# Block sums of weights on GpSimd, operand loads on its queue, and a final norm in columns, in a one-core decoder layer

## The chip, the cores and the metric

The kernel runs on one core of a Trainium2 chip. The metric is device time in microseconds (us) of one execution. All matrix work is single precision, emulated: each operand is split into a high and a low part, and TensorE does three products (high·high, high·low, low·high) for one.

## The reference, cut to what matters

One inference step of one layer on 520 tokens (512 of a prompt and 8 decode tokens), model width 2048, MLP width 8192:

```python
def block(x, ...):
    y, new = mixer(rmsnorm(x, w['g_mix']), ...)          # RG-LRU beside mLSTM; y = [...] @ w_out
    x = x + y
    x = x + cross_attn(rmsnorm(x, w['g_xattn']), mk, mv, w)   # w_cq, softmax over 256 memory tokens, w_co
    hf = rmsnorm(x, w['g_ffn'])
    x = x + jnp.square(jax.nn.relu(hf @ w['w_up'])) @ w['w_down']
    return x, new                                         # then a final rmsnorm of x
```

The 8 decode tokens have states of their own; the keys and values of the memory are results too.

## The kernel before, in words

A first part, to about 612 us, computes the input projection and the two recurrences. The rest is a row of matrix products with activations transposed (128 rows of features by 520 tokens): `out` (w_out), the memory's keys, `cq`, the memory's values, attention, `co`, `up`, and four groups of `down` (`d`).

**Strassen units.** `out`, `cq`, `co`, `up` and the `d` groups go through `strassen`, in 8, 8, 8, 32 and 4 x 8 = 88 units. A unit makes 256 output columns: its weights are four blocks A11, A21, A22, A12 of 128x1024, and it takes seven products, p0 to p6, in place of eight. The weight operand of each is a block or a sum of blocks, made by `weights(k, p)`:

- p0: A11
- p1: SS = A21 + A22, in a new tile
- p2: SS - A11 (and here also A21 becomes A11 - A21)
- p3: A12
- p4: the new A21
- p5: SS becomes A12 - SS
- p6: A22

The sums are `sub`, line 834, one VectorE instruction each. A product is 24 matmuls of 128x260 (line 955) into one of three PSUM banks, `acca`, `accb`, `accc`. The weight operand of product n + 2 (`LOOK`) is prepared while product n runs: `split_weights` makes `whi` on ScalarE (line 101) and `wlo` on VectorE (line 102). Blocks are loaded by `fetch` (line 889) on SP's queue, into a pool of seven tiles, which the sums share. A load waits until the last reader of its tile is done, and SP's queue goes in order.

**Operands.** The activation side has seven slots of two batches, each a high and a low tile. `batch_load` reads a batch from DRAM (line 858, on SP's queue as well), ScalarE casts it to the high part (line 859), and VectorE subtracts for the low part (line 854). The DRAM copies (`tdcq`, `tdup`, `tdd`) are written by `spill` (line 845) on GpSimd's queue, POOL. The last units of a stage are written straight into the operand tiles by `set_tail` (line 874).

**Results of a product.** `onto` adds a bank to an output tile (line 962, VectorE). In up, `blocks` copies it to `t` (line 973, ScalarE) or adds it (line 971, VectorE); after p6 come relu and square (lines 1355 and 1356), the operand's sums (`mixed`, line 834, on `w`), and the spill. `residual` stores the residual stream to `dx[2]` (line 995, POOL).

**scale_back.** While up runs, a side task computes two reciprocals by Ln and Exp (`negative_inverse`, lines 1318 to 1321; on ScalarE each Ln and Exp loads a table here), then takes the eight tiles of the residual stream, loads each (line 1341), multiplies it twice on VectorE (line 1345), and stores it (line 1346, POOL). It works with two tiles.

**Order.** A Tile scheduler puts the recorded instructions in order for each engine by priorities; preparation of weights, and evacuation, run ahead by 100 places. Each engine and each DMA queue then goes through its instructions in that order.

Of the kernel before, what the change touches and what calls it, by code (L numbers as in the profile page):

```python
# [9 lines left out]
F32 = mybir.dt.float32  # L10
F32R = mybir.dt.float32r
AF = mybir.ActivationFunctionType
# [33 lines left out]
def tile_trunk(ctx: ExitStack, tc: tile.TileContext, a, o):  # L46
# [71 lines left out]
    def start(gen, rate=None):  # L118

        tasks.append([gen, rate, 0.0])  # L120
# [677 lines left out]
    def rest():  # L798
# [22 lines left out]
        def tl(tag, shape, dt=F32):  # L821
            return stage[tag].tile(list(shape), dt, tag=tag, name=nm(tag))
# [10 lines left out]
        def sub(out, x, y, op=ALU.subtract):  # L833
            V.tensor_tensor(out=out, in0=x, in1=y, op=op)
# [20 lines left out]

        def batch_load(key, s, b, n=4):
            hi, lo = op_tile(), op_tile()
            load(lo[:, 0:n].bitcast(F32), td[key][b][:, s, 0:n])
            S.copy(hi[:, 0:n], lo[:, 0:n].bitcast(F32))  # L859
            lo_of(lo[:, 0:n], lo[:, 0:n].bitcast(F32), hi[:, 0:n])  # L860
            sets.setdefault((key, s), []).append((hi, lo))
# [449 lines left out]

        def up_enter():
            enter("d", x=2, r=1, t=2, w=2)()
            start(scale_back())

        def negative_inverse(y, t, v):

# [3 lines left out]
            V.scalar_tensor_tensor(out=y, in0=t, scalar=2.0, in1=y, op0=ALU.subtract, op1=ALU.mult)  # L1321

        def scale_back():
            for _ in range(16):
                yield

            va, vb = tl("x", (P, 2, T)), tl("x", (P, 2, T))
            v, y, t = va[:, 0], va[:, 1], vb[:, 0]
            mean_of(v)
            st["rphi"] = tl("r", (P, T))  # L1330
            negative_inverse(y, t, scl)
            V.scalar_tensor_tensor(out=st["rphi"], in0=y, scalar=-1.0, in1=v, op0=ALU.mult, op1=ALU.mult)
            yield
            negative_inverse(y, t, v)
            V.scalar_tensor_tensor(out=scl, in0=y, scalar=-1.0, in1=scl, op0=ALU.mult, op1=ALU.mult)
            yield
            for u in range(KB // 2):
                for _ in range(6):
                    yield
                x = tl("x", (P, 2, T))  # L1340
                load(x, dx[2][u])
                for _ in range(6):
                    yield
                for i in range(2):
                    V.tensor_tensor(out=x[:, i], in0=x[:, i], in1=st["rphi"], op=ALU.mult)
                store(dx[3][u], x)
# [12 lines left out]

        X = []  # L1360

        def down_load(u):
            x = tl("x", (P, 2 * T))
# [6 lines left out]
        def down_evac(u, p, box, last):  # L1370
            onto([st["X", u][:, 0], st["X", u][:, 1]], p, box["out"])
            if p == 6 and not last:
                store(dx[3][u], st["X", u])
            if last and p == 6:
                for n in (2 * u, 2 * u + 1):
                    if n == 0:
                        st["sc2"] = op_tile((P, T), F32)
                        V.scalar_tensor_tensor(out=st["sc2"], in0=scl, scalar=1.0 / D, in1=scl,
                                               op0=ALU.mult, op1=ALU.mult)
                        st["ss"] = tl("ss", (P, T))  # L1380
                        S.activation(st["ss"], X[n], AF.Square)
                    else:
                        for c in HALF:
                            sq = ax()[:, 0:HT]
                            S.activation(sq, X[n][:, c], AF.Square)
                            V.tensor_tensor(out=st["ss"][:, c], in0=sq, in1=st["ss"][:, c], op=ALU.add)

        def final():

            r, v, s_, q_ = (op_tile((P, T), F32) for _ in range(4))  # L1390
            for n in range(2, KB, 3):
                S.activation(X[n], X[n], AF.Copy, scale=pc(C_FIN, n))
            for c in HALF:
                ps = ax()
                PE.matmul(ps[:, 0:HT], ones, st["ss"][:, c], start=True, stop=True)
# [3 lines left out]
            S.activation(s_, s_, AF.Exp, scale=-0.5)  # L1399
# [3 lines left out]
            V.scalar_tensor_tensor(out=r, in0=q_, scalar=1.5, in1=s_, op0=ALU.add, op1=ALU.mult)  # L1403
            axs.close()
            with tc.tile_pool(name="pfin", bufs=1, space=PSUM, reuse_waits="tile") as pf:
                rp = pf.tile([P, 2, 512], F32, tag="rp", name="rp")[:, :, 0:HT]
                S.copy(rp, halves(r))
                for n in range(KB):
                    x = X[n]
                    if n % 3 == 2:  # L1410
                        G.tensor_tensor(out=x, in0=x, in1=r, op=ALU.mult)
                    else:
                        V.scalar_tensor_tensor(out=halves(x), in0=halves(x), scalar=pc(C_FIN, n), in1=rp,
                                               op0=ALU.mult, op1=ALU.mult)
                    (S.dma_start if n % 2 else load)(o["y"][n], x)
# [241 lines left out]
```

## Time and profile before

| | |
|---|---|
| median of three runs | 2793.49 us (2789.72 to 2793.79) |
| profiled execution | 2796.05 us, of which the span is 2794.2 |
| TensorE busy | 2665.4 us, 95% of the span |
| VectorE busy | 2245.1 us, 80% |
| ScalarE busy | 1437.9 us, 51% |
| GpSimd busy | 107.5 us, 4% |
| HBM read, written | 427.45 MB, 120.51 MB |

The stages by time in the trace: out from about 612 us, the memory's keys and cq from about 830, co to about 1415, up from there to about 2096, d to about 2769, then the final norm. In rows of the profile PE is TensorE, PEld its weight loads, DVE VectorE, ACT ScalarE, POOL GpSimd, SP the queue that only issues transfers. "DMA op<-tdup" is a load of an operand, "DMA raw<-in_w_up" a fetch of a weight block, "SPq L889" the time of SP's queue at that line. A clock of 1.00 is TensorE's full speed.

### The profile page before, as it was taken

The page shows a single profiled execution, that of the slowest core. Times are in us where ns is not written, and L with a number is a line of the kernel's source. Part 1 is how long each engine was busy: PE and PEld are TensorE (multiplying, and loading weights), DVE is VectorE, ACT ScalarE, POOL GpSimd, SP SyncE. Part 2 cuts the span into 40 slices and gives each one's busy share as a digit, 9 for nine tenths or more (in the row PEclk, how much of TensorE's full clock was granted, in tenths as well). Part 3 has the DMA queues.
Part 4 walks back from the last instruction along what each step waited for, and adds up shares of the span by engine and source line. Part 5 has one row for each costly group of instructions (what it writes and reads, how often), then busy time and mean ns, then how long its engine had stood idle before and what let it go on. Part 6 is the DMA issues. An engine that isn't in the chain of part 4 may idle for free.

```text
span 2794.2 us, 52079 instructions
## 1 busy us (share of the span) xinstructions
PE 2665.4 (95%) x21146; PEld 2613.6 (94%) x21146; DVE 2245.1 (80%) x3203; ACT 1437.9 (51%) x2114; POOL 107.5 (4%) x164
## 2 busy tenths in 40 slices
PE   8999999999999999889969999999999999999996
PEld 8999999999999998669969999999998999999996
DVE  7777788658887898789878777777878887978886
ACT  6445556525455467675455455545554353434543
POOL 0000000030000000000000000000000000000000
PEclk9999999999999999999989999999999999999998
DMA  4666643377676579976666545454457465654632
GB/s 169 196 211 213 196 148 94 99 272 275 220 247 227 202 229 324 335 256 210 198 216 228 174 145 168 151 162 157 159 198 258 164 238 168 222 186 161 223 109 81
DMA packets 178857, 551.24 MB, mean 197 GB/s; under 512 B 23725, under 2 KB 33645, under 8 KB 178617
## 3 DMA queue, kind: packets, MB, share of 16 engines
q1 hardware_dynamic: 152808, 453.61, 48.9%
q0 software_dynamic: 24080, 90.50, 9.0%
q8 instruction: 166, 2.72, 0.4%
q10 hardware_dynamic: 1728, 3.80, 0.4%
q14 instruction: 75, 0.61, 0.1%
HBM read 427.45 MB, written 120.51 MB: 196 GB/s over the span
## 4 chain that ended last, share of the span: by engine, by line
PE 36%; issue 16%; DMA 4%; DVE 2%; ACT 2%; POOL 1%; SPq 0%; POOLq 0%; DVEq 0%; ACTq 0%
PE acca L955 19%; PE accc L955 9%; PE accb L955 5%; PE mv L1202 2%; PE ax L185 1%; DMA op<-dq 1%; DMA x<-dx 1%; DMA dx<-x 1%; DVE wlo L102 1%; DVE op L854 0%; DMA kv<-in_V 0%; ACT kv L1159 0%; PE row L1129 0%; DMA tdup<-w 0%; DMA op<-tdup 0%
## 5 line engine op out<-in xcount | busy, mean ns | idle before, releaser
L955 PE MATMUL acca<-op,whi 128*128 128x260 f32 x5632 | 1037.3, 285 | 33.2 <-ACT t L973 10.3
L955 PEld LDWEIGHTS acca<-op,whi 128*128 128x128 f32 x5632 | 877.7, 190 | 38.1 <-ACT whi L101 11.9
L955 PE MATMUL acca<-op,wlo 128*128 128x260 f32 x2816 | 801.9, 285 | 4.5 <-DVE wlo L102 4.4
L101 ACT CAST whi<-raw 128x1024 fp32r<-128x1024 f32 x388 | 406.8, 1050 | 426.7 <-PE acca L955 148.8
L955 PEld LDWEIGHTS acca<-op,wlo 128*128 128x128 f32 x2816 | 535.4, 190 | 6.1 <-DVE wlo L102 6.1
L102 DVE TENSOR_TENSOR wlo<-raw,whi 128x1024 fp32r<-128x1024 f32 x388 | 473.5, 1222 | 77.4 <-ACT whi L101 73.7
L955 PE MATMUL accc<-op,whi 128*128 128x260 f32 x2816 | 518.5, 284 | 1.4 <-ACT whi L101 1.3
L101 ACT CAST whi<-raws 128x1024 fp32r<-128x1024 f32 x264 | 276.9, 1049 | 369.2 <-PE accc L955 110.0
L166 PE MATMUL mm<-xa,whi 128*128 128x260 f32 x2624 | 432.9, 286 | 11.1 <-ACT whi L101 8.3
L955 PEld LDWEIGHTS accc<-op,whi 128*128 128x128 f32 x2816 | 438.1, 189 | 2.7 <-ACT whi L101 1.8
L102 DVE TENSOR_TENSOR wlo<-raws,whi 128x1024 fp32r<-128x1024 f32 x264 | 322.9, 1223 | 121.5 <-ACT whi L101 120.8
L955 PE MATMUL accc<-op,wlo 128*128 128x260 f32 x1408 | 400.2, 284 | 0.9 <-DVE wlo L102 0.9
L166 PEld LDWEIGHTS mm<-xa,whi 128*128 128x128 f32 x2624 | 365.0, 190 | 13.7 <-ACT whi L101 8.3
L955 PE MATMUL accb<-op,whi 128*128 128x260 f32 x1408 | 262.1, 286 | 8.4 <-ACT op L859 4.6
L955 PEld LDWEIGHTS accc<-op,wlo 128*128 128x128 f32 x1408 | 266.5, 189 | 1.3 <-DVE wlo L102 1.2
L166 PE MATMUL mm<-xa,wlo 128*128 128x260 f32 x1312 | 266.2, 284 | 0.0
L955 PEld LDWEIGHTS accb<-op,whi 128*128 128x128 f32 x1408 | 219.6, 190 | 9.8 <-ACT op L859 4.8
L166 PEld LDWEIGHTS mm<-xa,wlo 128*128 128x128 f32 x1312 | 203.9, 190 | 0.7 <-DVE wlo L102 0.5
L955 PE MATMUL accb<-op,wlo 128*128 128x260 f32 x704 | 200.8, 285 | 0.4 <-DVE wlo L102 0.3
L854 DVE TENSOR_TENSOR op<-op,op 128x1040 fp32r<-128x1040 f32 (+3 forms) x136 | 159.9, 1180 | 36.5 <-ACT op L859 22.0
L859 ACT CAST op<-op 128x1040 fp32r<-128x1040 f32 (+1 forms) x112 | 111.9, 1007 | 90.1 <-DMA op<-tdd 55.0
L101 ACT CAST whi<-wraw 128x1024 fp32r<-128x1024 f32 x82 | 85.5, 1043 | 122.8 <-PE mm L166 99.9
(386 smaller groups left out, 3355.0 us busy)
## 6 DMA issues: line engine op xcount, KB each, us to landing
raw<-in_w_up SPq DMA_DIRECT2D x128, 512.0 KB, 3.4
raw<-in_w_down SPq DMA_DIRECT2D x100, 512.0 KB, 4.1
wraw<-in_w_in SPq DMA_DIRECT2D x79, 512.0 KB, 4.0
tdd<-w POOLq DMA_DIRECT2D x32, 1040.0 KB, 6.3
x<-dx SPq DMA_DIRECT2D x56, 520.0 KB, 5.5
op<-tdd SPq DMA_DIRECT2D x56, 520.0 KB, 5.2
dx<-x POOLq DMA_DIRECT2D x48, 520.0 KB, 4.9
raw<-in_w_mk SPq DMA_DIRECT2D x32, 512.0 KB, 5.3
```

The costliest lines, as they stand in the source:

```text
L101: S.copy(hi, raw)
L102: V.tensor_tensor(out=lo, in0=raw, in1=hi.bitcast(F32), op=ALU.subtract)
L166: PE.matmul(ps[:, hf, 0:HT], w[:, j, :], x[:, HALF[hf]], start=(k == 0 and wi == 0), stop=(k == n - 1 and wi == 2))
L185: PE.matmul(out, u, v, start=first and i == 0, stop=last and i == 2)
L854: V.tensor_tensor(out=lo, in0=src, in1=hi.bitcast(F32), op=ALU.subtract)
L859: S.copy(hi[:, 0:n], lo[:, 0:n].bitcast(F32))
L955: PE.matmul(out, u[:, k], x[:, j], start=(new and k == 0 and i == 0), stop=(k == 7 and i == 2), skip_group_check=not new)
L1202: PE.matmul(st["mv"][i], x[:, ms], u[:, j], start=(k == 0 and wi == 0), stop=(k == KB - 1 and wi == 2))
```

## The change

1. `batch_load` for cq and up issues on POOL's queue in place of SP's (14 loads each).
2. In `weights`, the sum A11 - A21 moves from p2 on VectorE to p3 on GpSimd, and A12 - SS from p5 on VectorE to p3 on GpSimd, two products sooner. Both are still 128x1024 with two SBUF inputs. VectorE has 3003 rows after, 3175 before; POOL 373 and 169.
3. `scale_back` starts at p6 of unit 2 of up, its first ScalarE instructions behind that unit's square, in place of the entry of up and 16 steps. One reciprocal comes ahead of the mean.
4. The final norm's factor is computed on [128, 5] columns (one number a token): one-column matmuls against `ones`, five small VectorE operations, Sqrt in place of Ln and Exp with its table loaded early by a dummy, and six matmuls that spread the columns over 128x520 in PSUM (`rp`). VectorE's eleven multiplications read `rp`; GpSimd's five read a copy. The columns `scol`, `sc2`, `esc` are made in the last group of d.

```diff
-            load(lo[:, 0:n].bitcast(F32), td[key][b][:, s, 0:n])
+            (store if key in ("cq", "up") else load)(lo[:, 0:n].bitcast(F32), td[key][b][:, s, 0:n])
...
             elif p == 2:
-                sub(R(A21), R(A11), R(A21))
                 sub(R(SS), R(SS), R(A11))
-            elif p == 5:
-                sub(R(SS), R(A12), R(SS))
+            elif p == 3:
+                G.tensor_tensor(out=R(A21), in0=R(A11), in1=R(A21), op=ALU.subtract)
+                G.tensor_tensor(out=R(SS), in0=R(A12), in1=R(SS), op=ALU.subtract)
...
         def up_enter():
             enter("d", x=2, r=1, t=2, w=2)()
-            start(scale_back())
...
         def scale_back():
-            for _ in range(16):
-                yield
...
+            with tc.issue_after(st["mark"].ins):
+                negative_inverse(y, t, scl)
             mean_of(v)
-            st["rphi"] = tl("r", (P, T))
-            negative_inverse(y, t, scl)
...
-                S.activation(w[:, 0:4], t, AF.Square)
+                ins = S.activation(w[:, 0:4], t, AF.Square)
+                if u == 2:
+                    st["mark"] = ins
+                    start(scale_back())
...
-                        st["sc2"] = op_tile((P, T), F32)
...
+                        columns(ps, [scl], ident)
...
+                        with tc.issue_after(ins.ins):
+                            S.activation(cols[:, 3], ones[:, 0:NCH + 1], AF.Sqrt)
...
-            for c in HALF:
-                ps = ax()
-                PE.matmul(ps[:, 0:HT], ones, st["ss"][:, c], start=True, stop=True)
-                V.tensor_tensor(out=v[:, c], in0=ps[:, 0:HT], in1=st["sc2"][:, c], op=ALU.mult)
-            V.tensor_tensor(out=v, in0=v, in1=esc, op=ALU.add)
-            S.activation(s_, v, AF.Ln)
-            S.activation(s_, s_, AF.Exp, scale=-0.5)
-            S.activation(q_, s_, AF.Square)
-            V.tensor_tensor(out=s_, in0=s_, in1=scl, op=ALU.mult)
+            columns(ps, [st["ss"]], ones)
+            V.tensor_tensor(out=v, in0=ps[:, 0:NCH + 1], in1=st["sc2"], op=ALU.mult)
+            V.tensor_tensor(out=v, in0=v, in1=st["esc"], op=ALU.add)
+            S.activation(s_, v, AF.Sqrt)
+            V.reciprocal(s_, s_)
+            V.tensor_tensor(out=q_, in0=s_, in1=s_, op=ALU.mult)
...
-                S.copy(rp, halves(r))
+                            PE.matmul(rp[:, h, o_:o_ + b_ - a_], rc[:, c:c + 1].to_broadcast([P, P]),
+                                      ident[:, a_ - c * CH:b_ - c * CH], start=True, stop=True)
...
+                S.copy(halves(r), rp)
```

Where it moves instructions, by the order on each engine. First the entry of up: SP's queue before, from the last fetches of co. The names are tiles with their numbers; `tdup_120` and `tdup_121` are the two batches of up's operands in DRAM, `raw` the weight blocks.

```order
L889 DMA raw_16217<-in_w_up 128x1024
L889 DMA raw_16219<-in_w_up 128x1024
L858 DMA op_16208<-tdup_120 128x1040
L889 DMA raw_16300<-in_w_up 128x1024
L858 DMA op_16213<-tdup_121 128x780
L889 DMA raw_16509<-in_w_up 128x1024
L858 DMA op_16252<-tdup_120 128x1040
L889 DMA raw_16544<-in_w_up 128x1024
L858 DMA op_16257<-tdup_121 128x780
L858 DMA op_16291<-tdup_120 128x1040
L858 DMA op_16296<-tdup_121 128x780
L889 DMA raw_16546<-in_w_up 128x1024
```

The same place on POOL's queue after; `dx` rows are stores of the residual stream, line 845 is the spill of co's unit 6, L911 and L912 are the two sums, of co's unit 7 (`raws_16128`) and of up's units 0 and 1.

```order
L858 DMA op_16207<-tdup_120 128x1040
L996 DMA dx_6_152<-x_15970 128x1040
L845 DMA tdup_121<-w_16159 1024x1x260
L912 TENSOR_TENSOR raws_16128<-raw_16038,raws_16128 128x1024
L858 DMA op_16212<-tdup_121 128x780
L911 TENSOR_TENSOR raw_16216<-raw_16171,raw_16216 128x1024
L858 DMA op_16253<-tdup_120 128x1040
L858 DMA op_16258<-tdup_121 128x780
L858 DMA op_16292<-tdup_120 128x1040
L996 DMA dx_7_153<-x_16203 128x1040
L858 DMA op_16297<-tdup_121 128x780
L858 DMA op_16334<-tdup_120 128x1040
```

The loads stood between fetches of weight blocks; now they stand between stores and sums, and SP's queue has the fetches alone. Further on, an SS sum stands ahead of slot 3's second batch, and an A21 sum ahead of slot 4's.

Second, POOL while scale_back runs, before (units 0 to 4 of up; the `dx` rows are scale_back's stores):

```order
L1346 DMA dx_1_155<-x_17707 128x1040
L845 DMA tdd_0_122<-w_16729 1024x1x260
L1346 DMA dx_2_156<-x_18091 128x1040
L1346 DMA dx_3_157<-x_18490 128x1040
L1346 DMA dx_4_158<-x_18887 128x1040
L1346 DMA dx_5_159<-x_19281 128x1040
L845 DMA tdd_0_122<-w_16956 1024x1x260
L1346 DMA dx_6_160<-x_19669 128x1040
L1346 DMA dx_7_161<-x_20069 128x1040
L845 DMA tdd_0_122<-w_17198 1024x1x260
```

and after (from the sum for unit 4):

```order
L911 TENSOR_TENSOR raw_17234<-raw_17190,raw_17234 128x1024
L1345 DMA dx_0_154<-x_17476 128x1040
L1345 DMA dx_1_155<-x_17859 128x1040
L912 TENSOR_TENSOR raws_17394<-raw_17304,raws_17394 128x1024
L845 DMA tdd_0_122<-w_17425 1024x1x260
L911 TENSOR_TENSOR raw_17466<-raw_17432,raw_17466 128x1024
L1345 DMA dx_2_156<-x_18258 128x1040
L1345 DMA dx_3_157<-x_18656 128x1040
L1345 DMA dx_4_158<-x_19048 128x1040
L1345 DMA dx_5_159<-x_19437 128x1040
L912 TENSOR_TENSOR raws_17623<-raw_17533,raws_17623 128x1024
L845 DMA tdd_1_123<-w_17654 1024x1x260
```

The stores come some four units later, and the sum for p5 of unit 5 stands behind four of them.

Third, VectorE in a steady unit before (unit 3 of up into unit 4; `w` rows are the sums of the operand that is spilled):

```order
L102 TENSOR_TENSOR wlo_17399<-raws_17396,whi_17398 128x1024
L834 TENSOR_TENSOR raws_17396<-raws_17396,raw_17205 128x1024
L102 TENSOR_TENSOR wlo_17439<-raws_17396,whi_17438 128x1024
L834 TENSOR_TENSOR w_17427<-w_17427 128x520
L834 TENSOR_TENSOR raws_17396<-raw_17303,raws_17396 128x1024
L834 TENSOR_TENSOR w_17427<-w_17427 128x260
L102 TENSOR_TENSOR wlo_17474<-raw_17303,whi_17473 128x1024
L834 TENSOR_TENSOR w_17427<-w_17427 128x260
L102 TENSOR_TENSOR wlo_17504<-raw_17240,whi_17503 128x1024
L834 TENSOR_TENSOR raws_17626<-raw_17469,raw_17471 128x1024
L834 TENSOR_TENSOR raw_17469<-raw_17434,raw_17469 128x1024
L102 TENSOR_TENSOR wlo_17539<-raws_17396,whi_17538 128x1024
```

and after, some units on:

```order
L102 TENSOR_TENSOR wlo_17856<-raws_17853,whi_17855 128x1024
L834 TENSOR_TENSOR raws_17853<-raws_17853,raw_17661 128x1024
L102 TENSOR_TENSOR wlo_17897<-raws_17853,whi_17896 128x1024
L834 TENSOR_TENSOR w_17886<-w_17886 128x520
L834 TENSOR_TENSOR w_17886<-w_17886 128x260
L102 TENSOR_TENSOR wlo_17934<-raw_17763,whi_17933 128x1024
L834 TENSOR_TENSOR w_17886<-w_17886 128x260
L102 TENSOR_TENSOR wlo_17964<-raw_17698,whi_17963 128x1024
L834 TENSOR_TENSOR raws_18085<-raw_17927,raw_17929 128x1024
L102 TENSOR_TENSOR wlo_17995<-raws_17853,whi_17994 128x1024
```

The SS sum behind the split of p2 and the A21 sum behind the next unit's p1 sum are gone from VectorE; what is left stands in the same order.

More of the change, by code (lines that the diff above doesn't have):

```diff
@@ L1398, in final @@
-            S.activation(s_, v, AF.Ln)
-            S.activation(s_, s_, AF.Exp, scale=-0.5)
-            S.activation(q_, s_, AF.Square)
-            V.tensor_tensor(out=s_, in0=s_, in1=scl, op=ALU.mult)
+            v, s_, q_, rc = (cols[:, 3 + i] for i in range(4))
+            ps = ax()
+            columns(ps, [st["ss"]], ones)
+            V.tensor_tensor(out=v, in0=ps[:, 0:NCH + 1], in1=st["sc2"], op=ALU.mult)
+            V.tensor_tensor(out=v, in0=v, in1=st["esc"], op=ALU.add)
+            S.activation(s_, v, AF.Sqrt)
@@ L1402, in final @@
+            V.reciprocal(s_, s_)
+            V.tensor_tensor(out=q_, in0=s_, in1=s_, op=ALU.mult)
             V.scalar_tensor_tensor(out=q_, in0=q_, scalar=-0.5, in1=v, op0=ALU.mult, op1=ALU.mult)
-            V.scalar_tensor_tensor(out=r, in0=q_, scalar=1.5, in1=s_, op0=ALU.add, op1=ALU.mult)
+            V.scalar_tensor_tensor(out=rc, in0=q_, scalar=1.5, in1=s_, op0=ALU.add, op1=ALU.mult)
+            V.tensor_tensor(out=rc, in0=rc, in1=st["scol"], op=ALU.mult)
             axs.close()
             with tc.tile_pool(name="pfin", bufs=1, space=PSUM, reuse_waits="tile") as pf:
-                rp = pf.tile([P, 2, 512], F32, tag="rp", name="rp")[:, :, 0:HT]
-                S.copy(rp, halves(r))
+                rp = pf.tile([P, 2, 512], F32, tag="rp", name="rp")
+                for c in range(NCH):
+                    for a_, b_ in ((c * CH, min((c + 1) * CH, HT)), (max(c * CH, HT), (c + 1) * CH)):
+                        if a_ < b_:
+                            h, o_ = a_ // HT, a_ - a_ // HT * HT
+                            PE.matmul(rp[:, h, o_:o_ + b_ - a_], rc[:, c:c + 1].to_broadcast([P, P]),
+                                      ident[:, a_ - c * CH:b_ - c * CH], start=True, stop=True)
+                PE.matmul(rp[:, 1, TP - HT:T - HT], rc[0:NB, NCH:NCH + 1].to_broadcast([NB, P]),
+                          ident[0:NB, 0:NB], start=True, stop=True)
+                rp = rp[:, :, 0:HT]
+                S.copy(halves(r), rp)
```

14 lines of the change are left out of this document (11 added, 3 removed).

## The prediction

> **What bounds the kernel.** I read the page first, then what TensorE waits for, then busy time by stretch, and last the chain and the queues at the entry of the up-projection, where the waits led. From the page:
>
> ```profile
> span 2794.2 us, 52079 instructions
> PE 2665.4 (95%) x21146; PEld 2613.6 (94%) x21146; DVE 2245.1 (80%) x3203; ACT 1437.9 (51%) x2114; POOL 107.5 (4%) x164
> ```
>
> TensorE works for 95% of the span, and the diff takes no matmul off it but in the tail. All that can be won is the 129 us in which it stands still. TensorE's waits (total, times, longest, in us), the three that matter here:
>
> ```profile
> PE acca L955 <- ACT t L973: 10.3, 2, 10.1
> PE accb L955 <- ACT op L859: 4.6, 1, 4.6
> PE ax L257 <- DVE ss L1002: 2.1, 1, 2.1
> ```
>
> The first two are single waits of 10.1 and 4.6, so they belong to one place and not to each unit. By stretch (length, then busy time of PE, PEld, DVE, ACT, POOL):
>
> ```profile
> 1748.00:1950.00 202.00, 202.00 (x1684) 202.00 (x1684) 156.33 (x171) 103.94 (x131) 8.46 (x10) 1.00 0.49 158
> 1405.00:1470.00 65.00, 41.69 (x279) 39.83 (x278) 49.31 (x64) 38.01 (x51) 1.62 (x3) 0.82 0.57 208
> 1260.00:1380.00 120.00, 120.00 (x1000) 119.91 (x999) 107.96 (x141) 60.98 (x74) 8.45 (x12) 1.00 0.63 206
> ```
>
> In the steady up stage (first row) TensorE has no gap, and VectorE is free for 46 of 202 us: work taken from it there is worth nothing. The same holds in the out-projection of cross-attention (third row), where VectorE is 90% busy. The entry of up (second row) loses 23 us of TensorE, and its granted clock, 0.82 there against 1.00, stretches what is left. Starts of the last product of a unit, from the timeline (first row, last unit of co) and the chain (up units 0, 2, 4, 5):
>
> ```profile
> 1411.65 0.48 PE L955 MATMUL acca<-op,whi 128*128 128x260 f32 x2 [1.77 <-DVE x L962]
> ```
>
> ```profile
> 1460.98 4.68 PE acca L955 x24
> ...
> 1505.54 6.01 PE acca L955 x48
> ...
> 1546.13 5.77 PE acca L955 x48
> ...
> 1566.31 5.77 PE acca L955 x48
> ```
>
> An undisturbed unit is 1566.31 - 1546.13 = 20.18. Unit 0 of up takes 49.33, so 29.2 are lost; units 1 and 2 take 44.56 against 40.36, so 4.2 more. Part of the 29.2 is the clock: the product at 1460.98 lasts 4.68, and an undisturbed one, half of the 5.77 of two, 2.88.
>
> **The change, part by part.** *Operand loads on POOL's queue.* The chain at that entry:
>
> ```profile
> 1396.77 9.31 DMA tdup<-w
> 1406.22 3.07 DMA op<-tdup
> ...
> 1437.90 1.24 DVE wlo L102
> 1439.15 0.33 SPq L889
> ...
> 1440.06 5.26 DMA op<-tdup
> 1445.34 1.06 ACT op L859
> ...
> 1448.02 1.28 ACT L1318
> ...
> 1453.40 5.12 DMA x<-dx
> ```
>
> The load that lands at 1445.34 had its source since 1406. It stood in SP's queue behind a weight fetch (L889), whose buffer came free when VectorE ended a `wlo` at 1439.15. That is the 10.1 wait: ScalarE does the cast at 1445.34 first, then the copy of `t` on which TensorE waits. On POOL's queue no load stands behind a fetch. It stands behind other things: the store of `dx2[7]`, which needs the last residual of co (about 1415), and GpSimd's sums, of which the order has five among the fourteen loads or just ahead. Costs from the groups of VectorE and GpSimd (count, busy us, mean ns):
>
> ```profile
> L834 DVE TENSOR_TENSOR raw<-raw,raw 128x1024 f32<-128x1024 f32 x81 | 98.9, 1222 | 1.1
> L834 DVE TENSOR_TENSOR raws<-raw,raws 128x1024 f32<-128x1024 f32 x81 | 98.9, 1221 | 0.7
> L854 DVE TENSOR_TENSOR op<-op,op 128x1040 fp32r<-128x1040 f32 x99 | 122.0, 1238 | 22.3 <-ACT op L859 17.7 <-ACT op L1226 4.6
> ```
>
> ```profile
> L1411 POOL TENSOR_TENSOR x<-x,op 128x520 f32<-128x520 f32 x5 | 6.2, 1274 | 175.3 <-DVE op L1403 175.3
> ```
>
> GpSimd's 1274 for 520 elements scale to 2.5 us for 1024. Five sums are 12.5, and fourteen issues at 0.55 (the store rows below) some 8: 20 us of POOL work, which fits a window of 35. What is late next is VectorE. It is busy 49.3 of 65 us, which makes 37.4 in the 49.33 of unit 0; five sums (6.1) and scale_back's first rows (some 3) leave it, so 28 remain, and of its present 12 us of waits for casts and landings (49.33 - 37.4) I let it keep 8 to 10, since the casts of 14 loads and the co tail stay. So unit 0 would take 36 to 38 from 1411.65, and its last product would start at 1448 to 1450, against 1460.98. I take **-12**; ends: -6 (the loads gain only the 5.26 landing and a cast, since POOL releases them late too) and -18 (half of VectorE's remaining waits go as well; at -29 nothing would be lost, which the casts and subtractions of 14 loads exclude). The loads of cq's operands have the same form; from the waits above the ax row's 2.1 is before the loads and stays. **-1.5**, ends -4 and +1.
>
> *scale_back later.* It started in unit 0 of up and now starts in unit 2, after its activation. The 4.2 lost in units 1 and 2 should go, and a similar loss can come back in units 3 to 6, where GpSimd's sums stand between the stores. Chain rows before, one round of a pair of tiles, and two of the stores on POOL:
>
> ```profile
> 1479.55 1.23 DVE x L1345 x2
> ...
> 1481.07 5.96 DMA dx<-x
> 1487.10 3.45 DMA x<-dx
> ```
>
> ```profile
> 1474.97 0.55 POOL L1346 DMA_DIRECT2D dx<-x  x1 [0.62 <-DVE x L1345]
> 1490.03 0.53 POOL L1346 DMA_DIRECT2D dx<-x  x1 [8.43 <-DVE x L1345]
> ```
>
> A round is 1.2 + 0.3 + 6.0 + 3.4 and a wait for VectorE: 15 us from pair to pair. VectorE's order now puts the multiplications of the pairs half a unit apart, 10 us, between the `wlo` of the running products; each VectorE row behind a multiplication that waits for its load is late by up to 3 to 5 us. Three rounds, of which VectorE's 23% of free time absorbs part: **+4**, ends 0 and +10. With the -4.2, **0**.
>
> *The sums on GpSimd.* 88 units, two sums each (81 of each kind in the rows above, seven more of each in the units that take other buffers): 176 x 1.22 = 215 us leave VectorE, 176 x 2.5 = 440 us come to GpSimd, 5 us of a 20.18 us unit. Beside a full TensorE the first is worth nothing. Does the second come late? Rows of a steady unit, from VectorE's and TensorE's timelines:
>
> ```profile
> 1652.37 1.23 DVE L102 TENSOR_TENSOR wlo<-raws,whi 128x1024 fp32r<-128x1024 f32 x1 [1.89 <-ACT whi L101]
> ...
> 1655.60 1.22 DVE L102 TENSOR_TENSOR wlo<-raw,whi 128x1024 fp32r<-128x1024 f32 x1
> ```
>
> ```profile
> 1658.60 0.28 PE L955 MATMUL accb<-op,wlo 128*128 128x260 f32 x1
> ```
>
> SS can be overwritten once the split of product 2 has read it, 1653.6; 2.5 later is 1656.1. Its own split (product 5) begins two products on, some 2.4 us after that, so the sum is early. The A21 sum stands behind the unit's spill, almost a unit ahead of its use. The split of product 3, which ran in between at 1655.60, is needed by 1658.60. **0**, +2 for entries of stages where slack is short; ends -3 and, if VectorE and GpSimd keep each other out, +35 (rival).
>
> The Trainium skill speaks against this part: in "SBUF — State Buffer", section "Who interferes with whom", a VectorE instruction with two SBUF inputs contends with a GpSimd instruction that reads SBUF, and the second of them waits for the whole of the first. Every `wlo` and sum here is of that kind. By that rule the 5.0 us of GpSimd per unit would be taken from VectorE's 202.00 - 156.33 free us in ten units; no row of before shows the two side by side, since L1411 runs beside a multiplication with one SBUF input.
>
> *Tail.* Before, the norm goes over 128x520 tiles; now over five columns:
>
> ```profile
> 2770.12 1.15 PE L1395 MATMUL ax<-ss,ones 128*128 128x260 f32 x4 [1.41 <-DVE ss L1386]
> ...
> 2773.15 1.28 ACT L1399 ACT_TABLE_LOAD   x1
> ...
> 2778.49 7.42 DVE L1413 SCALAR_TENSOR_TENSOR x<-x,par,rp 128x520 f32<-128x520 f32 x11 [0.66 <-ACT rp L1407]
> ```
>
> The old path was 2778.49 - 2770.12 = 8.4. Rows for the new one, from the timeline at the entry of cq and from VectorE's and ScalarE's groups:
>
> ```profile
> 838.55 3.33 PE L257 MATMUL ax<-ones,ss 128*128 128x1 f32 x24 [2.06 <-DVE ss L1002]
> ```
>
> ```profile
> L1051 DVE SCALAR_TENSOR_TENSOR nv<-ax,ne 128x5 f32<-128x5 f32 x1 | 0.2, 159 | 0.0
> ```
>
> ```profile
> L206 ACT ACTIVATE nrs<-nv 128x5 f32<-128x5 f32 x1 | 0.2, 208 | 0.6 <-DVE nv L1051 0.6
> ```
>
> The new path: columns of one tile instead of two, 1.7 (half of 3.33) plus 0.3 to release VectorE; seven small VectorE operations and one of ScalarE at 0.16 to 0.21 each, 1.3, and 0.6 for two changes of engine; six broadcast matmuls some 1.2 (estimate, as the six column matmuls less their wait); release 0.3. Sum 5.4, so **-3**; ends -1.5 and -4.5. GpSimd gets its copy about as long after VectorE as before, and its 6.25 us end before VectorE's 7.42.
>
> *Others.* The d stage's loads stay on SP; fewer VectorE rows at its entries, -1, ends -2 and +2.
>
> Sum: -12 - 1.5 + 0 + 2 - 3 - 1 = -15.5. The profiled execution took 2796.05 (span 2794.2 and 1.9 around it) and lies 2.6 above the median of 2793.49; against the median 2778.
>
> **Rivals.** *The two engines keep each other out (slower).* Place: each of 88 units, around product 3. If a sum starts at 1653.6 and VectorE's next two-input rows wait until 1656.1, the `wlo` that began at 1655.60 comes behind one delayed row and ends at 1657.4 to 1659, against 1658.60: from nothing to 0.4 us per unit. From 15.5/88 = 0.18 us per unit on, the gain is gone; at 0.4, +35: 2813. In co it would be worst, since 107.96 - 6 x 2.44 + 6 x 5.0 = 123 us of 120 would be occupied. No row speaks for it, and none excludes it, since the two kinds of instruction do not meet before. Against: in up 15.6 - 2.4 + 5.0 = 18.2 of 20.18 still fit, and splits are made two products ahead. By the rule of "SBUF — State Buffer" the keeping out itself is certain, and only whether the slack holds is open.
>
> *The loads only change queues.* dx_7's store waits for the last residual of co, and a GpSimd sum for a split: loads behind them come late as they did behind fetches. Entry gain 5 instead of 12, scale_back +3: 2788, no change to be seen.
>
> *scale_back blocks.* The stores of four tiles stand ahead of SS of unit 5 on POOL; if a multiplication waits a whole round, that sum, its split and product 5 are late, 5 us twice: 2788 likewise.
>
> *The entry empties.* All of -18, tail -4.5, cq -4: 2768.
>
> **How the numbers follow.** 0.2% of 2793, 5.6 us, is about what a measurement can tell from no change. Forecast (2770 to 2787): 0.62. Loads or scale_back give half back (2785 to 2791): 0.14, half of it within 0.2%. The entry empties: 0.08. Lock or another loss in steady units: 0.16, of which 0.04 merely eats the gain (2788 to 2799) and 0.12 is slower. Faster 0.62 + 0.06 + 0.08 = 0.76; within 0.2% 0.12; slower 0.12. The range, 2767 to 2797, leaves out most of the lock rival and the last bit below.
>
> **What would show it.** Right: the 10.1 wait on `t` L973 gone; unit 0 of up 36 to 39 us long; no TensorE gap from 1748 to 1950's counterpart, GpSimd's sums 2.5 us each; VectorE's last eleven multiplications beginning about 5.5 after the last sum of squares. Wrong: `wlo` rows whose length or start shifts by GpSimd's 2.5 and a TensorE wait on `wlo` L102 that grows with the number of units; loads on POOL issued later than 1440's counterpart; waits of TensorE around units 4 and 5 of up.

## The result, and the profile after

The change made the kernel slower: 2857.75 us, median of 2851.5 to 2859.4, against 2791.6 (2781.53 to 2793.79); ratio 1.0244, interval 1.0224 to 1.0264. The profiled execution has a span of 2857.6, 63.4 more than before. The page after, the lines that answer to those of before:

```profile
span 2857.6 us, 52462 instructions
PE 2690.3 (94%) x21178; PEld 2633.3 (92%) x21178; DVE 2333.4 (82%) x3030; ACT 1436.5 (50%) x2112; POOL 596.2 (21%) x368
```

VectorE lost 176 sums of 1.22 us, 215 us of work, and its busy time grew by 88 us. TensorE computes nothing more to speak of and is busy 25 us longer. What it waits for after:

```profile
PE acca L956 <- DVE x L963: 29.5, 15, 4.5
PE acca L956 <- ACT t L974: 13.7, 3, 10.2
PE acca L956 <- DVE wlo L102: 11.8, 9, 2.8
PE accc L956 <- DVE wlo L102: 9.5, 7, 2.8
```

The wait of ten microseconds on `t` is still there. New is the first row: 15 waits of some two microseconds each for `x` L963, the addition of a product to its output tile (before, two waits, 2.2 us in all). By stretch, co's units, the entry of up, and the steady up stage:

```profile
1260.00:1456.00 196.00, 172.11 (x1331) 169.40 (x1330) 161.89 (x185) 90.25 (x120) 51.26 (x35) 0.94 0.54 185
1456.00:1510.00 54.00, 36.42 (x238) 35.07 (x239) 36.69 (x45) 28.78 (x40) 11.53 (x13) 0.78 0.42 152
1620.00:2141.00 521.00, 521.00 (x4344) 521.00 (x4342) 432.92 (x388) 272.39 (x341) 179.35 (x78) 1.00 0.50 161
```

Steady up is full as before, with 179 us of GpSimd beside it. Co was full before and isn't now. VectorE's groups say why. Before:

```profile
L102 DVE TENSOR_TENSOR wlo<-raw,whi 128x1024 fp32r<-128x1024 f32 x388 | 473.5, 1222 | 77.4 <-ACT whi L101 73.7
L962 DVE TENSOR_TENSOR x<-acca,x 128x260 f32<-128x260 f32 x192 | 81.5, 425 | 25.4 <-PE acca L955 21.5 <-DMA x<-dx 2.9
L834 DVE TENSOR_TENSOR w<-w 128x260 f32<-128x260 f32 x96 | 40.7, 424 | 0.1
L1002 DVE TENSOR_TENSOR ss<-ss,sq 128x1040 f32<-128x1040 f32 x14 | 17.3, 1236 | 0.0
```

and after (lines one higher):

```profile
L102 DVE TENSOR_TENSOR wlo<-raw,whi 128x1024 fp32r<-128x1024 f32 x388 | 576.7, 1487 | 61.1 <-ACT whi L101 59.9
L834 DVE TENSOR_TENSOR w<-w 128x260 f32<-128x260 f32 x96 | 105.1, 1095 | 1.1
L1003 DVE TENSOR_TENSOR ss<-ss,sq 128x1040 f32<-128x1040 f32 x14 | 41.4, 2959 | 0.0
L963 DVE TENSOR_TENSOR x<-acca,x 128x260 f32<-128x260 f32 x192 | 80.9, 421 | 27.1 <-PE acca L956 26.5
```

The same instructions on the same shapes take 1.2 to 2.6 times as long where both inputs lie in SBUF. The one that reads a PSUM bank (`acca`) and one SBUF tile, the last row, takes what it took.

One unit of co shows the whole mechanism. The rows are timelines: start, duration, engine, line, names, and the idle time before it. VectorE in a unit of co before:

```profile
1356.03 1.24 DVE L1002 TENSOR_TENSOR ss<-ss,sq 128x1040 f32<-128x1040 f32 x1
1357.18 0.42 DVE L962 TENSOR_TENSOR x<-acca,x 128x260 f32<-128x260 f32 x1
```

VectorE, GpSimd and TensorE after, each by itself:

```profile
1389.75 0.42 DVE L834 TENSOR_TENSOR w<-w 128x260 f32<-128x260 f32 x1
1390.09 3.43 DVE L1003 TENSOR_TENSOR ss<-ss,sq 128x1040 f32<-128x1040 f32 x1
1393.45 0.42 DVE L963 TENSOR_TENSOR x<-acca,x 128x260 f32<-128x260 f32 x1
```

```profile
1389.97 2.45 POOL L912 TENSOR_TENSOR raws<-raw,raws 128x1024 f32<-128x1024 f32 x1 [1.34 <-issue]
```

```profile
1391.74 0.28 PE L956 MATMUL accc<-op,wlo 128*128 128x260 f32 x1
1394.01 0.48 PE L956 MATMUL acca<-op,whi 128*128 128x260 f32 x2 [2.00 <-DVE x L963]
...
1395.34 0.42 PE L956 MATMUL acca<-op,wlo 128*128 128x260 f32 x1
...
1398.37 0.28 PE L956 MATMUL acca<-op,wlo 128*128 128x260 f32 x1
```

GpSimd's SS sum starts 0.12 us ahead of the addition of squares and ends at 1392.42. The addition, 1.24 us by itself, ends at 1393.52, 1.10 behind GpSimd's end: it was shut out until then. This is so throughout: of the fourteen additions of squares, the eleven that start beside a running sum take 3.42 to 3.43 us and end 1.10 behind its end, and the other three keep 1.24. Behind the addition in VectorE's queue stands `x` L963, which empties the bank that TensorE's product 2 writes next. TensorE stands for 2.00 us. Soon after it is slow: the first and last rows of the fence have matmuls of 0.28, the one at 1395.34 has 0.42, and so it goes until about 1398.1. The granted clock, the third number from the end, was 1.00 in the 3.41 us that hold the gap and 0.50 in the next 3.42:

```profile
1391.25:1394.66 3.41, 1.42 (x12) 1.24 (x11) 3.41 (x3) 1.05 (x1) 1.99 (x2) 1.00 0.45 139
1394.66:1398.08 3.42, 3.42 (x18) 3.42 (x17) 3.04 (x4) 0.00 (x0) 0.27 (x1) 0.50 0.99 382
```

That product takes 4.64 us by its first start and last end where its neighbours take 3.05. 2.0 + 1.6 is 3.6 us a unit, and most units of out and co are 23.9 us after, 20.2 to 20.3 before. Two gaps of the same length in co, 2.08 before 1292.77 and 1.99 before 1323.58, have no slow product behind them (one unit there is 22.4); the last section says what sets them apart.

Where the time went, by stage: in microseconds from the start of product 3 in one unit to that in another (d to the end of the last product), worked out from TensorE's timeline of one profiled execution each; the other kernels are the experiments below. The first part is the same program in all and varies by 7.5, which is how far single executions can be trusted. Those of the first experiment and of the tied kernel ran 4 and 9 us below their medians.

| stretch | before | after | sums on VectorE | sums only | squares through PSUM | scale_back tied |
|---|---|---|---|---|---|---|
| first part, to out | 675.3 | 671.7 | 670.2 | 670.2 | 672.9 | 667.8 |
| out | 224.5 | 244.8 | 221.9 | 249.6 | 229.2 | 221.5 |
| cq and attention | 358.5 | 363.8 | 357.8 | 366.6 | 360.3 | 357.5 |
| co, units 0 to 7 | 142.8 | 162.3 | 143.0 | 166.0 | 144.9 | 142.8 |
| co 7 to up 3 (entry) | 116.1 | 111.9 | 104.1 | 118.9 | 106.4 | 101.9 |
| up 3 to 6 | 60.5 | 73.9 | 68.6 | 60.5 | 75.1 | 61.4 |
| up 6 to 31 | 504.3 | 504.0 | 504.3 | 504.0 | 504.0 | 504.3 |
| d | 686.7 | 701.9 | 680.9 | 700.2 | 702.9 | 680.0 |
| behind the last product | 25.5 | 23.3 | 22.9 | 25.5 | 23.3 | 23.3 |

### The profile page after: what moved, and what is told of

Its sections match the earlier page's. It is cut to its first block, busy times and chain, and to the rows that moved or that the text cites. A ratio compares the mean times of both kernels' runs of the same rounds, so it can differ in the third digit from the quotient of the medians.

```text
span 2857.6 us, 52462 instructions
## 1 busy us (share of the span) xinstructions
PE 2690.3 (94%) x21178; PEld 2633.3 (92%) x21178; DVE 2333.4 (82%) x3030; ACT 1436.5 (50%) x2112; POOL 596.2 (21%) x368
## 5 line engine op out<-in xcount | busy, mean ns | idle before, releaser
L956 PE MATMUL acca<-op,whi 128*128 128x260 f32 x5632 | 1054.9, 288 | 59.4 <-DVE x L963 29.5
L956 PEld LDWEIGHTS acca<-op,whi 128*128 128x128 f32 x5632 | 892.6, 193 | 66.7 <-ACT whi L101 27.5
L956 PE MATMUL acca<-op,wlo 128*128 128x260 f32 x2816 | 810.5, 288 | 11.9 <-DVE wlo L102 11.8
L102 DVE TENSOR_TENSOR wlo<-raw,whi 128x1024 fp32r<-128x1024 f32 x388 | 576.7, 1487 | 61.1 <-ACT whi L101 59.9
L956 PEld LDWEIGHTS acca<-op,wlo 128*128 128x128 f32 x2816 | 543.4, 193 | 14.1 <-DVE wlo L102 14.0
L102 DVE TENSOR_TENSOR wlo<-raws,whi 128x1024 fp32r<-128x1024 f32 x264 | 394.3, 1494 | 127.7 <-ACT whi L101 126.9
L912 POOL TENSOR_TENSOR raws<-raw,raws 128x1024 f32<-128x1024 f32 x81 | 209.4, 2585 | 579.9 <-DVE wlo L102 442.7
L911 POOL TENSOR_TENSOR raw<-raw,raw 128x1024 f32<-128x1024 f32 x81 | 226.9, 2802 | 423.0 <-DVE raws L834 338.7
L854 DVE TENSOR_TENSOR op<-op,op 128x1040 fp32r<-128x1040 f32 (+3 forms) x136 | 183.8, 1355 | 47.6 <-ACT op L859 32.0
```

The costliest lines, as they stand in the source:

```text
L102: V.tensor_tensor(out=lo, in0=raw, in1=hi.bitcast(F32), op=ALU.subtract)
L854: V.tensor_tensor(out=lo, in0=src, in1=hi.bitcast(F32), op=ALU.subtract)
L911: G.tensor_tensor(out=R(A21), in0=R(A11), in1=R(A21), op=ALU.subtract)
L912: G.tensor_tensor(out=R(SS), in0=R(A12), in1=R(SS), op=ALU.subtract)
L956: PE.matmul(out, u[:, k], x[:, j], start=(new and k == 0 and i == 0), stop=(k == 7 and i == 2), skip_group_check=not new)
```

## The experiments

Theory A: a VectorE instruction with two SBUF inputs and a GpSimd instruction that reads SBUF keep each other out; out and co lose since the SS sum falls beside the addition of squares with a bank's evacuation behind it. Rival B: the loss comes from POOL's queue, which now carries loads, stores and sums.

**Sums back on VectorE, the rest of the change kept** (the base of most others):

```diff
             elif p == 2:
+                sub(R(A21), R(A11), R(A21))
                 sub(R(SS), R(SS), R(A11))
-            elif p == 3:
-                G.tensor_tensor(out=R(A21), in0=R(A11), in1=R(A21), op=ALU.subtract)
-                G.tensor_tensor(out=R(SS), in0=R(A12), in1=R(SS), op=ALU.subtract)
+            elif p == 5:
+                sub(R(SS), R(A12), R(SS))
```

> The changed kernel with both sums back on VectorE at their old places; loads on POOL's queue, the late scale_back and the tail in columns stay. Theory A (GpSimd's sums shut out VectorE's two-input instructions; in out and co the sum of squares is caught and TensorE waits 2 us and runs slow for a product): the 14 long units of 23.9 us go back to 20.2, and with no sum between the loads of up the 10 us wait at its entry goes too: 2770 to 2785 us. Rival B (the loss comes from POOL's queue, where loads and stores now share places): out and co stay above 22 us a unit, 2835 or more.

Measured: 2779.86 us (ratio 0.9968, 0.9954 to 0.9982, to before). Out and co are at 20.2 to 20.3 a unit behind their first units, as A has it; B falls. The wait of ten microseconds at the entry of up shrank to 5.6 and did not go. The rest of the change is worth -8, the sums +78.

**The sums alone**, in the kernel before (the same lines, the other way):

> The kernel before with only the two sums moved to GpSimd; loads on SP, early scale_back and the old tail. Theory A: units of out and co are 23.9 us, about +22 in each, and the entries of d lose some 15: 2840 to 2860 us. Rival B: below 2810.

Measured: 2865.63 us (1.0266, 1.0243 to 1.0289), +77 to before and a little above the range. The cost is the sums' own and adds to the rest; POOL's queue without the loads makes it no smaller.

**Squares through PSUM**, the changed kernel:

```diff
-                        sq = tl("sq", (P, 2 * T))
-                        S.activation(sq, flat(X), AF.Square)
-                        V.tensor_tensor(out=flat(st_["ss"]), in0=flat(st_["ss"]), in1=sq, op=ALU.add)
+                        for i in range(2):
+                            for c in HALF:
+                                sq = ax()[:, 0:HT]
+                                S.activation(sq, X[:, i, c], AF.Square)
+                                V.tensor_tensor(out=st_["ss"][:, i, c], in0=sq, in1=st_["ss"][:, i, c], op=ALU.add)
```

> The changed kernel with one edit: in out and co the squares go to PSUM in halves of 260, so that the addition to ss has one SBUF input in place of two. The sums stay on GpSimd. Theory A: an addition with one SBUF input isn't shut out, it stays at 0.42 us, and the units of out and co fall from 23.9 to 20.2-20.8: 2800 to 2815 us. If GpSimd shuts out every VectorE instruction, or if the lateness is that of the sum itself: units stay at 23 or more, 2850 to 2860.

Measured: 2822.46 us (1.0115, 1.0087 to 1.0143), above the range by 7, but units of out and co are 20.1 to 20.3 behind the first of each. The addition, from VectorE's groups, and the GpSimd sum beside it:

```profile
L1005 DVE TENSOR_TENSOR ss<-ax,ss 128x260 f32<-128x260 f32 x56 | 22.4, 420 | 0.0
```

```profile
L912 POOL TENSOR_TENSOR raws<-raw,raws 128x1024 f32<-128x1024 f32 x81 | 210.3, 2596 | 581.1 <-DVE wlo L102 457.5 <-issue 96.1 <-DMA op<-tdco 13.8
```

With one SBUF input it isn't stretched at all, though the sums are still there, and 35 us come back from fourteen instructions. What stays is the entries, units 3 to 6 of up, and d.

**Only A21 on GpSimd:**

> The changed kernel with A11 - A21 on GpSimd and A12 - SS back on VectorE at p5. Theory A: only the SS sum falls beside the sum of squares, so units of out and co come back to 20.2-20.5; one A21 sum is left among the loads of up, and half of the stretching in d: 2780 to 2805 us. If each GpSimd sum costs alike: half of the loss stays, 2815 to 2830.

Measured: 2807.46 us (1.0056, 1.0035 to 1.0076), a miss by 2 above A's range. Units of out and co are 20.2 to 20.3 behind their first, and L1003 takes 1236 ns, so the two sums don't cost alike where they cost most. But one sum a unit still costs 28 against the first experiment, at the entries, in units 3 to 6 of up and in d.

**Sums in units 6 to 29 of up alone**, on the base of the first experiment:

> The kernel of the first experiment (sums on VectorE, the rest of the change kept) with the two sums on GpSimd in units 6 to 29 of up alone. Theory A: VectorE's `wlo` rows there are stretched, but nothing that TensorE needs within 2 us stands behind them: units stay at 20.2 us, the whole within 3 us of the first experiment, 2777 to 2783. If each GpSimd sum costs alike (78 us over 88 units): +21, 2800.

Measured: 2776.52 us (0.9955, 0.9937 to 0.9972), half a microsecond below A's range and far from the other. Busy time in that stage, and VectorE's groups there:

```profile
1700.00:2050.00 350.00, 350.00 (x2917) 350.00 (x2917) 290.36 (x264) 180.84 (x228) 114.60 (x51) 1.00 0.49 157
```

```profile
L102 DVE TENSOR_TENSOR wlo<-raw,whi 128x1024 fp32r<-128x1024 f32 x70 | 108.5, 1550 | 5.3 <-ACT whi L101 5.3
L834 DVE TENSOR_TENSOR w<-w 128x260 f32<-128x260 f32 x36 | 50.6, 1407 | 0.6
```

The stretching is as strong here as anywhere (424 ns became 1407), and TensorE doesn't notice.

**Sums in d alone:**

> The kernel of the first experiment with the two sums on GpSimd in the four groups of d alone. Theory A: d loses at its entries and beside its operand loads what it lost in the changed kernel, 4 to 6 us a group: 2796 to 2806 us. If only the sum of squares matters: 2778 to 2785.

Measured: 2800.54 us (1.0038, 1.0026 to 1.005), +21 to the first experiment, in A's range. TensorE's largest waits on `wlo` during d, in the first experiment and in this one (where matmuls are line 962):

```profile
PE acca L955 <- DVE wlo L102: 6.2, 7, 1.8
```

```profile
PE acca L962 <- DVE wlo L102: 11.2, 8, 2.8
PE accc L962 <- DVE wlo L102: 4.8, 2, 2.8
```

It is a handful of waits near the entries of groups. The three longest, of 2.8 each, have a slow product behind them, most of the shorter ones have none. A bank is late once (0.9); else it is the splits themselves.

**What in a GpSimd instruction shuts VectorE out?** Two runs put another instruction in the place of the SS sum of the changed kernel. First a write alone:

```diff
-                G.tensor_tensor(out=R(SS), in0=R(A12), in1=R(SS), op=ALU.subtract)
+                G.memset(R(SS), 0.0)
```

> The changed kernel with the SS sum on GpSimd replaced by a memset of the same tile at the same place (so product 5 takes zeros: this leaves out part of the computation). If only a GpSimd instruction that reads SBUF shuts out VectorE, as the Trainium skill has it ("SBUF — State Buffer", "Who interferes with whom"): the addition to ss stays at 1.24 us though the memset runs beside it, units of out and co 20.2-20.5, 2795 to 2812 us. If any GpSimd work does: it grows by the memset's length, units 21-23.

Measured, in a single execution: 2800.93 us, in the first range, units of out and co 20.2 to 20.5 behind their first. The two engines at one place:

```profile
1352.05 0.95 POOL L912 MEMSET raws<- 128x1024 f32 x1 [1.32 <-DVE wlo L102]
```

```profile
1352.18 1.24 DVE L1003 TENSOR_TENSOR ss<-ss,sq 128x1040 f32<-128x1040 f32 x1
```

They run side by side and the addition is not stretched, here or at any of the fourteen places (1.23 to 1.24). Then a read of one input, `G.tensor_copy(R(SS), R(A12))` in the same line:

> The changed kernel with the SS sum on GpSimd replaced by a copy of A12 into the same tile at the same place (product 5 takes A12: this leaves out part of the computation). One SBUF input in place of two. If reading is enough: the addition to ss ends 1.1 to 1.2 us behind the copy's end, so it grows by what is left of the copy when it starts, and units of out and co are long by that and a slow product, 21.5-24. If only two-input GpSimd instructions do it: 20.2.

Measured, in a single execution: 2817.28 us, units mostly 21.0, just below the range given. The same place:

```profile
1365.21 1.12 POOL L912 COPY raws<-raw 128x1024 f32<-128x1024 f32 x1 [1.33 <-issue]
```

```profile
1365.34 2.08 DVE L1003 TENSOR_TENSOR ss<-ss,sq 128x1040 f32<-128x1040 f32 x1
```

The addition ends at 1367.42, 1.09 behind the copy's end, as with the sum. One read is enough, and the stretch is what was left of GpSimd's instruction. The lateness of 0.8 makes units 0.8 longer and no more: TensorE's gaps there, mostly 0.6, brought no slow product.

**scale_back.** With the sums out of the way, units 3 to 5 of up are still long (68.6 in place of 60.5). Three runs, all on the base of the first experiment. First its old place, from the entry of up:

> The kernel of the first experiment with scale_back where it was before (from the entry of up). If its late place costs the 8 us by which units 3 to 5 are long there, and its early place 3 to 8 at the entry: 2773 to 2782 us. If the late place costs nothing in sum: 2780 to 2788.

Measured: 2783.72 us (0.9986, 0.9974 to 0.9997). Units 3 to 6 take 60.5, and the entry 114.8 in place of 104.1: the late place gains 10.7 there and gives 8.1 back later. The whole lies in the second range, 4 above the first experiment with intervals that overlap. Then more steps around each load (11 in place of 6, twice):

> The kernel of the first experiment with eleven steps in place of six before and behind each load of scale_back, so that a tile comes every 22 products' steps and not every twelve. If units 3 to 5 are long since VectorE's multiplications wait for a load that has not landed and hold what is behind them: these units come back to 20.2-21 and the whole to 2770 to 2776 us. If scale_back's own work is what costs: 2778 to 2784.

Measured: 2780.43 us (0.9981, 0.9964 to 0.9998); units 3 to 6 take 68.1. That lies in the second range, but decides nothing, since the edit did not change what it was to change: the steps set the order of recording, and the scheduler put the multiplications as early in VectorE's order as before (the first three pairs start 90.9, 98.0 and 104.1 us behind product 3 of unit 0, and 90.9, 97.9 and 104.0 in the first experiment). The rows show the wait all the same, VectorE's and then TensorE's:

```profile
1559.58 1.31 DVE L1343 TENSOR_TENSOR x<-x,r 128x520 f32<-128x520 f32 x2 [4.71 <-DMA x<-dx]
1560.81 1.22 DVE L102 TENSOR_TENSOR wlo<-raws,whi 128x1024 fp32r<-128x1024 f32 x1
```

```profile
1562.08 0.39 PE L955 MATMUL acca<-op,wlo 128*128 128x260 f32 x1 [2.41 <-DVE wlo L102]
```

So the third ties the order itself:

```diff
-                V.tensor_tensor(out=t[:, i], in0=out, in1=t[:, i], op=ALU.add)
+                st["vm"] = V.tensor_tensor(out=t[:, i], in0=out, in1=t[:, i], op=ALU.add)
...
-                for i in range(2):
-                    V.tensor_tensor(out=x[:, i], in0=x[:, i], in1=st["rphi"], op=ALU.mult)
+                with tc.issue_after(st["vm"].ins):
+                    for i in range(2):
+                        V.tensor_tensor(out=x[:, i], in0=x[:, i], in1=st["rphi"], op=ALU.mult)
```

> The kernel of the first experiment with each pair of scale_back's multiplications held in VectorE's order behind the addition to t that stands at its place in the program, so that they come one tile in one to two units. If units 3 to 5 are long since VectorE waits at a multiplication for a load (up to 4.7 us in the experiment with more steps, which the scheduler's order undid) with a `wlo` behind it: those waits go, all units of up behind unit 0 take 20.2-20.5, and the whole is 2769 to 2775 us. If the work itself costs: 2776 to 2783.

Measured: 2771.76 us (0.9947, 0.9926 to 0.9967), in the range: the best version, 15 below before. Units 3 to 6 take 61.4, one of them 21.0, above the 20.5 given. TensorE's waits on `wlo` from about there to the end of up, with the multiplications tied and untied (first experiment):

```profile
PE acca L955 <- DVE wlo L102: 1.7, 1, 1.7
```

```profile
PE acca L955 <- DVE wlo L102: 4.3, 2, 2.2
```

**What the loads on POOL are worth:** the first experiment with the loads back on SP.

> The kernel of the first experiment with the operand loads of cq and up back on SP's queue, so that of the whole change the late scale_back and the tail are left. From the start of product 3 of co's last unit to that of up's unit 1 it was 73.1 us before, 72.3 with the loads on POOL and scale_back early, 63.8 with the loads on POOL and scale_back late. If each edit gives its own share at that entry: 72 to 73 here, since the queue alone would hold the loads. If only both together give it, as ScalarE's tables and SP's queue were each late enough for TensorE: 70 to 73 too, and the two can't be told apart by the loads' share. If scale_back alone gives it: 63 to 66. From product 3 of out's last unit to cq's first: 79 to 80 (79.7 before, 75 with the loads on POOL). The whole: 2784 to 2794 us, or 2778 to 2785 if scale_back alone gives the entry.

Measured: 2785.04 us (0.9998, 0.9977 to 1.0019). The entry to unit 1 takes 65.8, so scale_back's place alone gives most of it: of 73.1 - 63.8 = 9.3, the move gives 7.3 and the loads 2.0 (0.8 where scale_back stays early). The 2.0 is no larger than the spread of single executions: the same stretch, with the same program in it, takes 61.6 to 64.9 in five of these kernels. Into cq it is 81.2, a miss by 1 above the range, and 75.1 with the loads on POOL, so there they give some 5. The whole lies where the two ranges meet, so it is the entry that decides.

## Why the prediction was wrong

**The step that failed is "The sums on GpSimd", +2.** It measured +78 (2857.75 against 2779.86). The duration was right (2.5 us predicted, 2.45 in the unit shown, 2.59 and 2.80 in the mean of 81 of each kind), and so was the result for the place where the slack was worked out: a steady up unit lost nothing, 504.0 against 504.3 in 25 units. The error was to carry that unit's slack to all 88. In out and co a `w` sum stands behind the split of p2, and behind that, where up has a split, the addition of squares with the evacuation of a bank next to it; no slack there was looked up. The order of those units was as easy to read as that of up, and VectorE's 107.96 of 120 us in co was quoted as a warning and not followed.

**The rival that came true was priced by half.** That the two engines keep each other out had 0.16 of the chances, at +35 and "around product 3". The runs show 3.6 us a unit in out and co (about 42 between the changed kernel and the first experiment), none in steady up, 21 in d, and the rest at cq, in attention and in the two disturbed places of up. Two things were missing: that a shut-out instruction passes its delay to whatever stands behind it in the queue, harmless kinds as well, and that a gap of 2 us can be followed by a product at half the clock, 1.6 us more. So the signs of being wrong named a wait on `wlo`, and the largest that came was on `x` L963. The rule weighed, "SBUF — State Buffer" of the Trainium skill, section "Who interferes with whom", holds here in each part that was tried: two inputs against one (the addition of squares grew from 1236 to 2959 ns in the mean, its quarters with one SBUF input stayed at 420 each), reading against writing only (3.43 us beside the sum, 1.24 beside the memset), and the wait until the other's end. The prediction took the keeping out as certain by that rule, and gave the loss a sixth of the chances since it had found slack in the one kind of unit where it looked.

**"Operand loads on POOL's queue", -12, was right in sum and wrong in cause.** Without the sums the stretch from co 7 to up 3 is 12.0 shorter, but by the experiments the loads give some 2 of it, which is not clear of the spread, and scale_back's move the rest. The 10.1 wait on `t`, from which the term was read, is the end of a chain that other waits replace: with the loads on SP and scale_back late it is there again, 10.1, and the entry is short all the same.

**In the changed kernel most of that gain is lost to the rival of queues that only change.** POOL at the entry of up after, and then the chain there:

```profile
1478.07 3.03 POOL L911 TENSOR_TENSOR raw<-raw,raw 128x1024 f32<-128x1024 f32 x1 [5.43 <-DVE raws L834]
1481.06 2.69 POOL L858 DMA_DIRECT2D op<-tdup  x5
```

```profile
1482.68 6.96 DMA op<-tdup
...
1490.93 0.38 ACT t L974
1491.31 0.04 issue
1491.35 5.57 PE acca L956 x24
```

Five loads wait behind an A21 sum of unit 1, which waits 5.43 us for a sum on VectorE. The one that the chain goes through lands at 1489.64, and TensorE stands 10.24 us, as it did before behind SP's fetch. Co 7 to up 3 takes 111.9 in place of 104.1, and 116.1 before. Not the stores, which were named first, but the sums do it.

**scale_back, 0, measured** -2.7 in units 1 and 2 (43.0 to 40.3 in the first experiment, by product 3) and +8.1 in units 3 to 5, within the ends of 0 and +10 given for the latter; the mechanism, multiplications waiting for a load with splits behind them, is the one predicted. With the sums beside it the loss is 13.4.

**The tail, -3, measured -1.5** from the last product's end to the first multiplication (2768.71 to 2778.49 before, 2834.31 to 2842.58 after) and -2.2 to the end of the kernel. Its rows:

```profile
2835.72 1.40 PE L257 MATMUL ax<-ones,ss 128*128 128x1 f32 x12 [1.41 <-DVE ss L1399]
2838.92 2.47 PE L1425 MATMUL rp<-ident,od 128*128 128x128 f32 x10 [1.81 <-DVE od L1416]
2841.32 0.59 PE L1427 MATMUL rp<-ident,od 8*128 8x8 f32 x2
2841.95 0.59 ACT L1430 COPY op<-rp 128x520 f32<-128x520 f32 x1 [4.19 <-PE rp L1427]
2842.58 7.42 DVE L1436 SCALAR_TENSOR_TENSOR x<-x,par,rp 128x520 f32<-128x520 f32 x11 [3.80 <-ACT op L1430]
```

The matmuls that spread the columns take 3.0 and not 1.2: they are twelve rows, at a granted clock of 0.50. VectorE starts only when ScalarE's copy of `rp` has ended, though it reads `rp` itself. In the trace its one wait is for the semaphore that this copy raises, so the wait stands in the program; why the scheduler put it there is open. **cq, -1.5:** from out's last unit to cq's first it was about -4.6 with the loads on POOL (79.7 to 75.1), beyond the value taken. **d, -1,** for fewer VectorE rows at its entries, came out the other way: 701.9 against 686.7 before, +15.2, since the splits that TensorE waits for there are among the stretched instructions. Without the sums on GpSimd it was 680.9.

## What to carry to other kernels

Before work is moved to GpSimd, go through VectorE's order in every stage, and at each place where GpSimd will run note what stands behind the next instruction with two SBUF inputs: its whole delay goes to that, and from there to TensorE. Work in GpSimd costs nothing where the neighbours are early (25 units here) and 2 to 3.6 us a unit where a bank's evacuation is next. If it must run beside, give VectorE's neighbour one input from PSUM, and put no loads on a queue whose head can be a sum that waits.

## What the runs showed of the hardware that was not expected

- A gap of 2.0 us on TensorE can be enough for a lower clock: the granted clock, 1.00 in full stages, was 0.50 for 3.41 us behind it, and matmuls of 128x260 lasted 0.42 and not 0.28 us. Where the gap falls decides. In all fourteen traces the granted clock changes only on a grid of 3.41 us. Between 684 and 2750 us, all 167 steps of that grid at full clock in which TensorE was busy for less than 45% were followed by a step at 0.50, and of the 578 that were busy for 50% or more but not throughout, 12 were. A gap of 1.91 inside one step in out was enough; one of 2.08 in co, and one of 2.90 in the run with the memset, were split between two steps and were not. The long units of 23.9 us are seven steps, so a gap that falls badly once does so again in the next unit.
- A blocked VectorE instruction is recorded as a long one, not as idle time: busy time rises (2245.1 to 2333.4) while work falls. Means by group, against the kernel before, show it at once; the waits don't name GpSimd.
- GpSimd is shut out as well: its A21 sum takes 2.39 us in co, where no VectorE instruction with two SBUF inputs is under way when it starts, 2.80 in the mean of 81, and 3.03 at the entry of up, where it starts within such an instruction and ends 2.24 behind its end.
